# An encoder block on one core: a 320-byte tile ahead of the weights, and another order of the last sums and outputs

## The chip, the cores and the metric

The kernel runs on one core of a Trainium2 chip. The metric is the device time of one execution in microseconds (us); lower is better. The time before is 990.51 us, the median of three runs (989.64 to 991.15).

## The reference

One layer of an encoder over 256 tokens of width 2048, all in float32:

```python
h = rmsnorm(x, norm1_g)
proj = h @ w_in                               # q 1536 | k 512 | v 512 | u 512
a = rmsnorm(window_attention(q, k, v, sink), attn_out_g)   # 12 heads, 4 kv heads, |t-s| <= 128
f = rmsnorm(fourier_mix(u, w_fourier), fourier_out_g)
x = x + concatenate([a, f]) @ w_out
h = rmsnorm(x, norm2_g)
gate, val = split(h @ w_up)                   # 5504 columns each
gate = depthwise_conv3(gate, dw_w) + dw_b
x = x + (gelu(gate) * val) @ w_down
return rmsnorm(x, normf_g)
```

## The kernel before

**Products in two parts.** Every large product is made of float32 values split in two: `hi`, the value rounded to the type `float32r`, and `lo`, the rest. Three of the four partial products are summed: hi·hi, lo·hi and hi·lo. The tokens are kept turned and split, in four tiles `hT` of [128, 4, 512] (the tiles `hU` take their buffers after the first half of the layer): 256 columns hi and 256 columns lo side by side for each block of 128 features.

**Units.** The weights come in 24 units for `w_in` (4 for u, 4 for v, 16 for k and q), 16 for `w_out`, and for the feed-forward 86 for `w_up` (gate and value of 43 blocks of 128 columns) and 44 for `w_down` (11 groups of 4). A unit is 1 MB (768 KB in the last four), a tile of 128 partitions by 2048 float32. `load` issues its DMA from SyncE into one of three `raw` buffers; `split` makes `hi` on ScalarE (line 143) and `lo` on VectorE (line 144), two units ahead of TensorE.

**Two forms of matmul.** In `still_weights` (lines 293 and 294; k, q, gate, value) a unit's weights are the stationary operand. For each of 16 blocks there are two matmuls: `hi` against the 512 columns of a token tile, and `lo` against 256 columns of it. In `moving_weights` (lines 282 to 284; u, v, `w_out`, `w_down`) the weights stream, 512 columns at a time, and tokens, `cat` (the attention and Fourier outputs) or `act` (the activations) are stationary. A unit has 4 blocks, 2 token blocks and 3 partial products, so 24 matmuls. Each matmul instruction has its own weight load (PEld in the profile).

**Where tiles lie.** Pools are placed behind each other in the partitions of the on-chip memory, and tiles behind each other in their pool, with sizes rounded up to 32 bytes. `base` holds the residual `xs`, `hT` and small tiles; the weight pool `wp` (`raw`, `hi`, `lo`, `junk`) follows it, then `cat` and the attention's tiles, and in the feed-forward `fp` (with `act`) in their place. Each pair of one unit's operands is thus shifted against the other by the small tiles between them. Modulo 512 bytes, `hT` begins at 96 and `raw`, `hi`, `lo`, `cat` and `act` at 288.

**The end.** The order of instructions is written out by hand: each engine runs its own in the order of the code and waits for others through semaphores. The feed-forward alternates groups of 8 up units with 4 down units. The last down group has three blocks. Its eight products (column block c, token block b) come in the order (0,0), (0,1), (1,0), (1,1), (2,0), (3,0), (2,1), (3,1), the last in two halves of 256 columns (lines 941 to 943). `last_post` adds a product to the residual on VectorE (line 833), takes the sum of squares on ScalarE (`square_sum`, line 819) and, for c < 3, multiplies by the final gain on GpSimd (line 836). `most_of` adds the sums so far (`tot`, `part`), `last_scale` adds the last one (`var`) and takes the power -1/2 on GpSimd (`rstd`, line 854). `finish` scales the four column blocks of a token block, c = 0 and 1 on ScalarE (line 869), 2 and 3 on VectorE (lines 867 and 863), and issues their output DMAs from SyncE (line 870). `finish(0)` is recorded after product (2,1), ahead of the two halves of (3,1); `finish(1)` is last.

Of the kernel before, what the change touches and what calls it, by code (L numbers as in the profile page):

```python
# [8 lines left out]
F32 = mybir.dt.float32  # L9
F32R = mybir.dt.float32r  # L10
AF = mybir.ActivationFunctionType
ALU = mybir.AluOpType

P = 128
# [38 lines left out]
FF_GROUPS = [list(range(g * 4, min(g * 4 + 4, NF))) for g in range((NF + 3) // 4)]  # L53
# [3 lines left out]
def block_kernel(  # L57
# [17 lines left out]
    nc = tc.nc  # L75
    SL = slopes()
    ctx.enter_context(tc.manual_schedule())
    base = ctx.enter_context(tc.tile_pool(name="base", bufs=1))
# [7 lines left out]
    def bank(pool, name):  # L86
        return pool.tile([P, 512], F32, tag=pool.name, name=name)
# [24 lines left out]
    raws, halves = {}, {}  # L112
# [11 lines left out]
    def split(i, pieces=1):  # L124

        for _ in split_parts(i, pieces):
            pass
# [37 lines left out]
    xs = [base.tile([P, 2, 512], F32, tag=f"xs{c}", name=f"xs{c}") for c in range(4)]  # L165
# [60 lines left out]
    ps = bank(dn, "ps_warm")  # L226
# [49 lines left out]
    def moving_weights(hi, lo, n, kk, act, b, ps, first, last, q0=0):  # L276

        for q, k in enumerate(kk, q0):
            ah = act(k)[:, b * P : (b + 1) * P]
            al = act(k)[:, S + b * P : S + (b + 1) * P]  # L280
            wh, wl = hi[:, q * n : (q + 1) * n], lo[:, q * n : (q + 1) * n]
            nc.tensor.matmul(ps, ah, wh, start=first and q == q0, stop=False)  # L282
            nc.tensor.matmul(ps, al, wh, start=False, stop=False)  # L283
            nc.tensor.matmul(  # L284
                ps, ah, wl, start=False, stop=last and q == q0 + len(kk) - 1
            )
# [18 lines left out]
    def step(i, ahead=2):  # L305
        todo, later[:] = list(later), []
        for g in todo:
            next(g, None)
        split(i + ahead)
        for g in todo:  # L310
            for _ in g:
                pass
# [20 lines left out]
    for c in range(4):  # L333
        t = base.tile([P, 4, 512], F32R, tag=f"hT{c}", name=f"hT{c}")
        hT.append(t)
    ps_u = [bank(mm, f"ps_u{b}") for b in range(2)]
    for k in range(NK):
        c, q = k // 4, k % 4
# [4 lines left out]
        hi, lo = halves[c]  # L343
# [392 lines left out]
    for n, (c, kq) in enumerate(OUT_ORDER):  # L736
        i = N_OUT + n
# [14 lines left out]
        if kq >= 2:  # L752
            part = "a" if kq == 2 else "f"
            ps = ps_a[c] if kq < 3 else ps_a[c, "f"]
            last = c in added
# [15 lines left out]
    gfb = fp.tile([P, D], F32, tag="gfb", name="gfb", bufs=1)  # L771
    nc.gpsimd.dma_start(gfb, normf_g.partition_broadcast(P))
    hT[:] = hT2
    act = {}
# [42 lines left out]
    def square_sum(c, b, part, o, n):  # L817
        junk = wp.tile([P, 512], F32, tag="junk", name=f"junkc{c}{b}{part}")
        nc.scalar.activation(
            junk[:, 0:n], xs[c][:, b, o : o + n], AF.Square,  # L820
            accum_out=ssq3[:, b, part : part + 1],
        )

    def down_post(g, c, ps):
# [2 lines left out]
            nc.vector.tensor_tensor(xb, ps[b], xb, ALU.add)  # L827
        yield

    def last_post(c, b, ps, o=0, n=512, part=None):  # L830

        xb = xs[c][:, b, o : o + n]
        nc.vector.tensor_tensor(xb, ps, xb, ALU.add)
        square_sum(c, b, c if part is None else part, o, n)
        if c < 3:
            nc.gpsimd.tensor_tensor(
                xb, xb, gfb[:, c * 512 + o : c * 512 + o + n], ALU.mult
            )

    def most_of(b, n):  # L840

        tot = base.tile([P, 1], F32, tag=f"tot3{b}", name=f"tot3{b}")
        nc.vector.tensor_reduce(tot, ssq3[:, b, 0:n], mybir.AxisListType.X, ALU.add)
        var = base.tile([P, 1], F32, tag=f"part3{b}", name=f"part3{b}")
        nc.vector.tensor_scalar(var, tot, 1.0 / D, EPS, ALU.mult, ALU.add)
        return var

    def last_scale(b, n, var):
        v = base.tile([P, 1], F32, tag=f"var3{b}", name=f"var3{b}")
        nc.vector.scalar_tensor_tensor(  # L850
            v, ssq3[:, b, n : n + 1], 1.0 / D, var, ALU.mult, ALU.add
        )
        r = base.tile([P, 1], F32, tag=f"rstd3{b}", name=f"rstd3{b}")
        nc.gpsimd.tensor_tensor(r, v, half_pow[:, 0:1], ALU.pow)
        return r

    def finish(b, r):
        y = [
            fp.tile([P, 512], F32, tag="act", name=f"y{b}{c}", bufs=12) for c in range(4)
        ]  # L860
        for c in (0, 3, 1, 2):
            if c == 3:
                nc.vector.scalar_tensor_tensor(
                    y[c], xs[c][:, b, :], r, gfb[:, 1536:2048], ALU.mult, ALU.mult
                )
            elif c == 2:
                nc.vector.tensor_scalar(y[c], xs[c][:, b, :], r, None, ALU.mult)
            else:
                nc.scalar.activation(y[c], xs[c][:, b, :], AF.Copy, scale=r)
            nc.sync.dma_start(  # L870
                out[b * P : (b + 1) * P, c * 512 : (c + 1) * 512], y[c]
            )

    last = len(FF_GROUPS) - 1
    n = 0
    while n < len(ff_units):
        kind, g, j = ff_units[n]
        i = n_front + n
        if n == 0:
            pair = []  # L880
            for q in range(2):
                ps = bank(mm, f"ps_{ff_units[q][0]}{j}")
# [16 lines left out]
        hi, lo = halves.pop(i)  # L899
        if kind == "down" and g == last:  # L900
            break
        if kind == "down":
            ps = [bank(dn, f"ps_d{g}{j}{b}") for b in range(2)]
# [4 lines left out]
        else:  # L908
            ps = bank(mm, f"ps_{kind}{j}")
# [4 lines left out]


    halves[i] = (hi, lo)
    todo = []
    for c, b in [(0, 0), (0, 1), (1, 0), (1, 1), (2, 0), (3, 0), (2, 1), (3, 1)]:
        hi, lo = halves[i + c]
        ps = bank(dn, f"ps_e{c}{b}")  # L920
        if (c, b) != (3, 1):
            moving_weights(hi, lo, 512, FF_GROUPS[last], act.get, b, ps, True, True)
            todo.append((last_post, (c, b, ps)))
        if (c, b) in [(0, 1), (1, 0)]:
            step(i + c)
        if (c, b) != (0, 0):
            for f, a in todo:
                f(*a)
            todo = []
        if (c, b) == (3, 0):  # L930
            r3 = last_scale(0, 3, most_of(0, 3))
        if (c, b) == (2, 1):
            finish(0, r3)
    for p in range(2):
        ps = bank(dn, f"ps_e31{p}")
        for q, k in enumerate(FF_GROUPS[last]):
            o = q * 512 + p * 256
            ah, al = act[k][:, P:S], act[k][:, S + P : 2 * S]
            wh, wl = hi[:, o : o + 256], lo[:, o : o + 256]
            end = q == len(FF_GROUPS[last]) - 1  # L940
            nc.tensor.matmul(ps[:, 0:256], ah, wh, start=q == 0, stop=False)
            nc.tensor.matmul(ps[:, 0:256], al, wh, start=False, stop=False)
            nc.tensor.matmul(ps[:, 0:256], ah, wl, start=False, stop=end)
        last_post(3, 1, ps[:, 0:256], p * 256, 256, 3 + p)
        if p == 0:
            var = most_of(1, 4)
    finish(1, last_scale(1, 4, var))


def _layout(inp):  # L950
# [90 lines left out]
```

## Time and profile before

| | |
|---|---|
| median of three runs | 990.51 us (989.64 to 991.15) |
| the profiled execution's own time | 989.97 us |
| its span, first to last instruction | 988.2 us |
| granted TensorE clock, mean | 0.998 |
| TensorE busy | 977.0 us, 99% |
| weight loads busy | 838.2 us, 85% |
| VectorE, ScalarE, GpSimd busy | 696.1, 466.5, 23.6 us |
| DMA | 186.42 MB, mean 189 GB/s |

The profile names engines PE (TensorE), PEld (its weight loads), DVE (VectorE), ACT (ScalarE), POOL (GpSimd) and SP (SyncE). L12 is line 12 of the kernel. Tiles are given as out<-in. A row of the timeline has the start and the duration in us, the engine, the line, the operation, tiles, shapes and count, and in brackets the idle time before it and what ended it. A row of the view of stretches has the stretch, its length, and for each engine the busy time and in brackets the instructions.

### The profile page before, as it was taken

The page shows a single profiled execution, that of the slowest core. Times are in us where ns is not written, and L with a number is a line of the kernel's source. Part 1 is how long each engine was busy: PE and PEld are TensorE (multiplying, and loading weights), DVE is VectorE, ACT ScalarE, POOL GpSimd, SP SyncE. Part 2 cuts the span into 40 slices and gives each one's busy share as a digit, 9 for nine tenths or more (in the row PEclk, how much of TensorE's full clock was granted, in tenths as well). Part 3 has the DMA queues.
Part 4 walks back from the last instruction along what each step waited for, and adds up shares of the span by engine and source line. Part 5 has one row for each costly group of instructions (what it writes and reads, how often), then busy time and mean ns, then how long its engine had stood idle before and what let it go on. Part 6 is the DMA issues. An engine that isn't in the chain of part 4 may idle for free.

```text
span 988.2 us, 12858 instructions
## 1 busy us (share of the span) xinstructions
PE 977.0 (99%) x5185; PEld 838.2 (85%) x5185; DVE 696.1 (70%) x935; ACT 466.5 (47%) x587; POOL 23.6 (2%) x35
## 2 busy tenths in 40 slices
PE   9999999999999999999999999999999999999996
PEld 7788898888888888888888888888888888888885
DVE  6658877575687776767767767777677677676764
ACT  6756666544454434444434444344344343443434
POOL 0000000000000000000000000000000000000003
PEclk9999999999999999999999999999999999999999
DMA  9844443445545555464555555555545455555542
GB/s 330 341 178 153 148 165 134 171 170 205 221 170 178 204 178 206 172 213 171 191 192 180 204 182 201 184 196 177 210 170 208 175 192 192 178 206 190 193 128 86
DMA packets 30091, 186.42 MB, mean 189 GB/s; under 512 B 3408, under 2 KB 3920, under 8 KB 9040
## 3 DMA queue, kind: packets, MB, share of 16 engines
q1 hardware_dynamic: 29744, 184.54, 52.9%
q8 instruction: 41, 0.67, 0.3%
q0 software_dynamic: 144, 1.05, 0.3%
q14 instruction: 18, 0.15, 0.0%
q10 hardware_dynamic: 144, 0.01, 0.0%
HBM read 183.49 MB, written 2.10 MB: 188 GB/s over the span
## 4 chain that ended last, share of the span: by engine, by line
PE 98%; DMA 1%; issue 0%; SPq 0%; ACT 0%; POOL 0%; DVE 0%; ACTq 0%; POOLq 0%
PE ps_gate L293 16%; PE ps_val L293 16%; PE ps_val L294 8%; PE ps_gate L294 8%; PE ps_d L284 7%; PE ps_d L283 7%; PE ps_d L282 7%; PE ps_q L293 5%; PE ps_q L294 2%; PE ps_a L284 2%; PE ps_a L282 2%; PE ps_a L283 2%; PE ps_k L293 2%; PE ps_o L642 1%; PE ps_s L570 1%; PE ps_k L294 1%
## 5 line engine op out<-in xcount | busy, mean ns | idle before, releaser
L144 DVE TENSOR_TENSOR lo<-raw,hi 128x2048 fp32r<-128x2048 f32 (+3 forms) x178 | 388.4, 2182 | 97.7 <-ACT hi L143 97.7
L143 ACT ACTIVATE hi<-raw 128x2048 fp32r<-128x2048 f32 (+3 forms) x177 | 324.3, 1832 | 166.6 <-PE ps_d L283 106.0
L293 PE MATMUL ps_gate<-hU,hi 128*128 128x512 f32 x688 | 242.6, 394 | 0.0
L293 PE MATMUL ps_val<-hU,hi 128*128 128x512 f32 x688 | 242.6, 394 | 0.0
L294 PE MATMUL ps_val<-hU,lo 128*128 128x256 f32 x688 | 193.0, 281 | 0.0
L294 PE MATMUL ps_gate<-hU,lo 128*128 128x256 f32 x688 | 193.0, 280 | 0.0
L293 PEld LDWEIGHTS ps_val<-hU,hi 128*128 128x128 f32 x688 | 129.4, 188 | 30.1
L293 PEld LDWEIGHTS ps_gate<-hU,hi 128*128 128x128 f32 x688 | 129.4, 188 | 30.0
L294 PEld LDWEIGHTS ps_gate<-hU,lo 128*128 128x128 f32 x688 | 128.9, 187 | 0.4
L294 PEld LDWEIGHTS ps_val<-hU,lo 128*128 128x128 f32 x688 | 128.9, 187 | 0.0
L284 PE MATMUL ps_d<-lo,act 128*128 128x512 f32 x320 | 124.6, 389 | 0.0
L283 PE MATMUL ps_d<-hi,act 128*128 128x512 f32 x320 | 124.6, 389 | 0.0
L282 PE MATMUL ps_d<-hi,act 128*128 128x512 f32 x320 | 124.5, 389 | 0.0
L780 ACT ACTIVATE ft_g<-ps_gate 128x256 f32<-128x256 f32 x43 | 16.5, 384 | 134.2 <-PE ps_gate L294 134.2
L827 DVE TENSOR_TENSOR xs<-ps_d,xs 128x512 f32<-128x512 f32 x80 | 54.5, 687 | 25.7 <-PE ps_d L284 25.7
L282 PEld LDWEIGHTS ps_d<-hi,act 128*128 128x128 f32 x320 | 60.1, 188 | 12.6
L284 PEld LDWEIGHTS ps_d<-lo,act 128*128 128x128 f32 x320 | 60.1, 188 | 12.5
L283 PEld LDWEIGHTS ps_d<-hi,act 128*128 128x128 f32 x320 | 60.1, 188 | 12.2
L293 PE MATMUL ps_q<-hT,hi 128*128 128x512 f32 x192 | 68.5, 397 | 0.0
L780 ACT ACTIVATE ft_v<-ps_val 128x256 f32<-128x256 f32 x43 | 16.5, 384 | 95.5 <-PE ps_val L294 95.5
L782 DVE TENSOR_TENSOR fa_g<-ps_gate,ft_g 128x256 f32<-128x256 f32 x43 | 18.2, 424 | 55.3 <-ACT ft_g L780 55.3
L294 PE MATMUL ps_q<-hT,lo 128*128 128x256 f32 x192 | 54.0, 281 | 0.0
(175 smaller groups left out, 1036.1 us busy)
## 6 DMA issues: line engine op xcount, KB each, us to landing
raw<-in_w_up SPq DMA_DIRECT2D x86, 1024.0 KB, 4.8
raw<-in_w_down SPq DMA_DIRECT2D x40, 1024.0 KB, 4.7
raw<-in_w_in SPq DMA_DIRECT2D x21, 1024.0 KB, 4.9
raw<-in_w_out SPq DMA_DIRECT2D x16, 1024.0 KB, 4.8
raw<-in_w_down_last SPq DMA_DIRECT2D x4, 768.0 KB, 4.2
raw<-in_w_in SPq DMA_DIRECT2D x8, 256.0 KB, 5.7
xs<-in_x SPq DMA_DIRECT2D x4, 512.0 KB, 10.8
out_y<-y SPq DMA_DIRECT2D x8, 256.0 KB, 2.5
```

The source lines that it names most:

```text
L143: nc.scalar.activation(hi[:, s], raw[:, s], AF.Copy)
L144: nc.vector.tensor_tensor(lo[:, s], raw[:, s], f32(hi[:, s]), ALU.subtract)
L282: nc.tensor.matmul(ps, ah, wh, start=first and q == q0, stop=False)
L283: nc.tensor.matmul(ps, al, wh, start=False, stop=False)
L284: nc.tensor.matmul(ps, ah, wl, start=False, stop=last and q == q0 + len(kk) - 1)
L293: nc.tensor.matmul(ps, hi[:, s], h, start=k == 0, stop=False)
L294: nc.tensor.matmul(ps[:, 0:S], lo[:, s], h[:, 0:S], start=False, stop=k == NK - 1)
L570: nc.tensor.matmul(ps[:, b * S : (b + 1) * S], qT[:, qo + b * P : qo + (b + 1) * P], kT[:, ko : ko + S], start=n == 0, stop=n == 2,)
L642: nc.tensor.matmul(ps[:, 0:S], v[:, sb, g * HD : (g + 1) * HD], pt[q][:, sb * S : (sb + 1) * S], start=sb == 0 and n == 0, stop=sb == 1 an ...
L780: nc.scalar.activation(tmp, ps[:, S : 2 * S], AF.Copy)
L782: nc.vector.tensor_tensor(add, ps[:, 0:S], tmp, ALU.add)
L827: nc.vector.tensor_tensor(xb, ps[b], xb, ALU.add)
```

## The change

1. A tile of 320 bytes a partition, `room`, is allocated in `base` behind the four token tiles. No instruction uses it. All tiles behind it move by 320 bytes, so the tokens stay at 96 modulo 512, and `raw`, `hi`, `lo`, `cat` and `act` begin at 96 as well.
2. The multiplication by the final gain becomes a function of its own, `gain`. `finish` becomes a generator that records one output at a time, in the order c = 0, 3, 2, 1. For token block 0, outputs 0 and 3 are recorded after product (2,1), output 2 after the first half of (3,1), and output 1 after the second half and after `most_of`. `most_of(1)` is recorded after the second half's addition and square instead of between the halves.

The order of TensorE's and GpSimd's instructions stays. The loop over the last products is written out.

```diff
+    base.tile([P, 80], F32, tag="room", name="room")
...
+    def gain(c, b):
+        xb = xs[c][:, b, :]
+        nc.gpsimd.tensor_tensor(xb, xb, gfb[:, c * 512 : (c + 1) * 512], ALU.mult)
...
         square_sum(c, b, c if part is None else part, o, n)
-        if c < 3:
-            nc.gpsimd.tensor_tensor(
-                xb, xb, gfb[:, c * 512 + o : c * 512 + o + n], ALU.mult
-            )
...
-        for c in (0, 3, 1, 2):
+        for c in (0, 3, 2, 1):
...
             nc.sync.dma_start(
                 out[b * P : (b + 1) * P, c * 512 : (c + 1) * 512], y[c]
             )
+            yield
...
+    r3 = last_scale(0, 3, most_of(0, 3))
+    last_post(2, 1, last_product(2, 1))
+    outs = finish(0, r3)
+    next(outs)
+    next(outs)
+    gain(2, 1)
+    hi, lo = halves[i + 3]
     for p in range(2):
...
         last_post(3, 1, ps[:, 0:256], p * 256, 256, 3 + p)
         if p == 0:
-            var = most_of(1, 4)
-    finish(1, last_scale(1, 4, var))
+            next(outs)
+    most = most_of(1, 4)
+    for _ in outs:
+        pass
+    for _ in finish(1, last_scale(1, 4, most)):
+        pass
```

More of the change, by code (lines that the diff above doesn't have):

```diff
@@ L916, in block_kernel, with last_product @@
     halves[i] = (hi, lo)
-    todo = []
-    for c, b in [(0, 0), (0, 1), (1, 0), (1, 1), (2, 0), (3, 0), (2, 1), (3, 1)]:
+    def last_product(c, b):
         hi, lo = halves[i + c]
         ps = bank(dn, f"ps_e{c}{b}")
[L921 to L933, printed above, removed]
+        moving_weights(hi, lo, 512, FF_GROUPS[last], act.get, b, ps, True, True)
+        return ps
+    held_ps = last_product(0, 0)
+    ps = last_product(0, 1)
+    step(i)
+    last_post(0, 0, held_ps)
+    last_post(0, 1, ps)
+    gain(0, 0)
+    gain(0, 1)
+    ps = last_product(1, 0)
+    step(i + 1)
+    last_post(1, 0, ps)
+    gain(1, 0)
+    for c, b in [(1, 1), (2, 0), (3, 0)]:
+        last_post(c, b, last_product(c, b))
+        if c < 3:
+            gain(c, b)
+    r3 = last_scale(0, 3, most_of(0, 3))
[5 more added lines that the diff above has]
+    hi, lo = halves[i + 3]
     for p in range(2):
```

## The prediction

> **What bounds the kernel now.** I read the page first (busy shares, slices, chain), then the busy time of each engine in chosen stretches, then the timeline of the last microseconds.
>
> ```profile
> PE 977.0 (99%) x5185; PEld 838.2 (85%) x5185; DVE 696.1 (70%) x935; ACT 466.5 (47%) x587; POOL 23.6 (2%) x35
> ...
> PEclk9999999999999999999999999999999999999999
> ...
> PE 98%; DMA 1%; issue 0%; SPq 0%; ACT 0%; POOL 0%; DVE 0%; ACTq 0%; POOLq 0%
> ```
>
> TensorE is busy 977.0 of the 988.2 us, at full clock in every slice, and is 98% of the chain that ended last. There is hardly a wait to remove. The time can only fall if matmuls follow each other at a shorter spacing, or if the part after the last matmul gets shorter. The change tries both: a 320-byte tile that moves operands in memory, and a new order of the last vector and scalar steps.
>
> For the first part I need the true spacing from one matmul's start to the next; the mean durations don't give it, since matmuls are pipelined and overlap in the trace. So I chose stretches that begin with the first matmul of a stage and end with the first of the next, and divide their length by the matmuls that the code issues in them.
>
> ```profile
> core 0: us, PE busy (x) PEld busy (x) DVE busy (x) ACT busy (x) POOL busy (x), PEclk, DMA share, GB/s
> 29.41:40.61 11.20, 11.20 (x50) 8.97 (x48) 3.71 (x4) 10.51 (x21) 0.71 (x1) 1.00 1.03 403
> 50.78:56.37 5.59, 5.59 (x27) 4.51 (x25) 2.95 (x2) 2.88 (x3) 0.00 (x0) 1.00 0.34 139
> 486.50:508.29 21.79, 21.79 (x99) 18.02 (x98) 15.21 (x15) 8.28 (x7) 0.00 (x0) 1.00 0.57 196
> 508.29:552.95 44.66, 44.66 (x258) 39.11 (x256) 32.42 (x41) 19.79 (x22) 0.00 (x0) 1.00 0.53 188
> 274.38:353.61 79.23, 79.23 (x452) 68.96 (x451) 62.66 (x84) 37.78 (x46) 0.00 (x0) 1.00 0.53 186
> 89.21:94.85 5.64, 5.64 (x35) 4.92 (x33) 5.25 (x16) 3.67 (x8) 0.00 (x0) 1.00 0.55 189
> ```
>
> Rows one and two are v units, row three four down units, rows four and five up units, row six one q unit. Put beside them where the operands lie. The allocator gives each tile a place in its partition; modulo 512 bytes, before the change, tokens (hT, hU) are at 96, and weights (hi, lo), the attention outputs (cat) and the activations (act) at 288. Each slice a matmul reads starts a multiple of 512 bytes further, so it has the same place.
>
> - Down (row three): 512 columns, both operands at 288. 21.79 us for 4 units of 24 matmuls: **227.0 ns** each.
> - v (rows one and two): the same instruction form, 512 columns, but tokens at 96 against weights at 288. 11.20 us / 48 = **233.3 ns** and 5.59 / 24 = **232.9 ns**. The two rows differ threefold in DMA (403 and 139 GB/s) and much in ScalarE (94% and 52% busy), and the spacing is the same. So it isn't traffic of others; what differs from down is which tiles are read, and where they lie.
> - Up and q: a 512-column matmul (tokens times hi) and a 256-column one (times lo), tokens at 96, weights at 288. 44.66 / 128 pairs = **348.9 ns**; in the first groups 79.23 / 224 = **353.7 ns**; in q 5.64 / 16 = **352.5 ns**.
>
> **Part 1, the 320 bytes.** `room` lies in the pool behind the tokens and ahead of the weights. Tokens stay at 96; weights, cat and act go from 288 to 96 (288 + 320 = 608). So after it the operands of u, v, q, k and up have one place, as those of down and of the output projection have now, and those of down and projection still have one place. Nothing is added to any engine. In the Fourier and attention parts nearly all pairs of tiles move together. What the landing places of the loads cost DMA is covered: its share is 0.53 to 0.57 in the feed-forward.
>
> The cost of a pair with one place isn't in the trace, since no stage mixes 512 and 256 columns at one place. I build it from its halves. The 512-column half is down's, 227.0 ns. For 256 columns at one place there are the last 18 matmuls (act and hi, both at 288):
>
> ```profile
> 976.55 0.28 PE L941 MATMUL ps_e<-hi,act 128*128 128x256 f32 x1
> 976.66 0.28 PE L942 MATMUL ps_e<-hi,act 128*128 128x256 f32 x1
> ...
> 978.58 0.28 PE L943 MATMUL ps_e<-lo,act 128*128 128x256 f32 x1
> ```
>
> From the second to the eighteenth 1.92 us for 16: 120.0 ns. The first follows a 512-column matmul and takes 0.11 us only. I take 120.0, from sixteen, and keep 0.113 for the range. Pair: 227.0 + 120.0 = **347.0 ns**.
>
> - 16 up units in the slow rhythm: 256 pairs x (353.7 - 347.0) = 1.7 us.
> - The other 70: 1120 x (348.9 - 347.0) = 2.1 us.
> - 16 q and k units: 256 x (352.5 - 347.0) = 1.4 us.
> - 8 u and v units: 192 matmuls x (232.9 - 227.0) = 1.1 us. I count half, 0.6: in the first v stretch ScalarE is 10.51 of 11.20 us busy and DMA at share 1.03, so they end next there.
>
> Sum **5.8 us**. In up nothing is late next: VectorE, the next busiest, works 32.42 of 44.66 us.
>
> The Trainium skill speaks against all of this: "TensorE: Matmul & The Clock Gate", Step-by-step, says that TensorE has two independent read ports, and that loading the next weights takes no read bandwidth from the running matmul. By it the relative place of the two operands would cost nothing, and this part would bring 0 instead of 5.8 us. The rows disagree so far: 232.9 and 233.3 ns against 227.0 with only tiles and places different.
>
> **Part 2, the end.** These rows carry it (the last matmul starts at 978.58, above):
>
> ```profile
> 977.36 0.74 DVE L863 SCALAR_TENSOR_TENSOR y<-xs,rstd,gfb 128x512 f32<-128x512 f32 x1
> 978.02 0.48 DVE L867 TENSOR_SCALAR y<-xs,rstd 128x512 f32<-128x512 f32 x1
> 978.17 1.32 ACT L869 ACTIVATE y<-xs,rstd 128x512 f32<-128x512 f32 x2
> 978.34 1.29 POOL L836 TENSOR_TENSOR xs<-xs,gfb 128x512 f32<-128x512 f32 x1 [1.17 <-ACT junkc L819]
> 978.41 0.42 DVE L833 TENSOR_TENSOR xs<-ps_e,xs 128x256 f32<-128x256 f32 x1
> 978.90 4.23 SPq L870 DMA_DIRECT2D out_y<-y  x5
> 979.39 0.40 ACT L819 ACTIVATE junkc<-xs 128x256 f32<-128x256 f32 x1
> 979.70 0.18 ACT L819 ACTIVATION_READ_ACCUMULATOR junkc<-xs 128x1 f32 x1
> 979.92 0.16 DVE L843 TENSOR_REDUCE tot<-ssq 128x1 f32<-128x4 f32 x1 [1.09 <-ACT junkc L819]
> 980.11 0.15 DVE L845 TENSOR_SCALAR part<-tot 128x1 f32<-128x1 f32 x1
> 980.18 0.41 DVE L833 TENSOR_TENSOR xs<-ps_e,xs 128x256 f32<-128x256 f32 x1
> 980.69 0.42 ACT L819 ACTIVATE junkc<-xs 128x256 f32<-128x256 f32 x1 [0.80 <-DVE xs L833]
> 981.23 0.16 DVE L850 SCALAR_TENSOR_TENSOR var<-ssq,part 128x1 f32<-128x1 f32 x1 [0.64 <-ACT junkc L819]
> 981.47 0.56 POOL L854 TENSOR_TENSOR rstd<-var,half_pow 128x1 f32<-128x1 f32 x1 [1.84 <-DVE var L850]
> 982.06 1.34 ACT L869 ACTIVATE y<-xs,rstd 128x512 f32<-128x512 f32 x2 [0.86 <-POOL rstd L854]
> ...
> L870 SPq DMA_DIRECT2D out_y<-y x8: 332/399/451, 978.9 to 984.2; - x8
> ```
>
> The last product is over by 978.86, but its addition (second L833) starts at 980.18. It stands behind the sum of squares (tot, part), which waits for ScalarE's square at 979.39, which stands behind two outputs of the first block (978.17, 1.32). The change takes one of these two outputs (c = 1) out of ScalarE's way and puts it behind both squares; on VectorE it orders: first addition, output c = 2, last addition, then tot and part. Replayed with the same durations:
>
> - VectorE: output c = 3 as now; first addition at 978.02; output c = 2 at 978.41; last addition at about 978.95, over at 979.36.
> - ScalarE: output c = 0 from 978.17 to 978.83; square of the first half to about 979.4; square of the second 0.1 us behind its addition (as 980.59 to 980.69 now), at 979.46; its sum reaches VectorE 0.54 us later (as 980.69 to 981.23): var at 980.00.
> - tot and part fit in from 979.43 to 979.75, ahead of that.
>
> var comes at 980.0 instead of 981.23: **1.2 us**. The moved output is then on ScalarE from 979.98 to 980.64; the scale of the second block (0.83 us behind var's start, 981.23 to 982.06) comes at 980.83. It hides by 0.2 us; without that cover the end slips by at most 0.66. Its DMA leaves SP's queue at 980.7 for some 0.4 us, ahead of the second block's first issue near 981.6. The multiplication by the gain on GpSimd (978.34, 1.29) keeps its place in its queue and is over at 979.63, before the power. The exchange of c = 1 and c = 2 in the second block changes nothing: four issues in a row set the end there, the last at 984.2, whichever tile comes third.
>
> **Sum.** 5.8 + 1.2 = 7.0 us. Against the profiled execution, 989.97 us: 983.0. That run lies 0.5 us under the median of 990.51, so the forecast is **983.5 us**.
>
> **The rivals.**
>
> 1. *The short matmuls gain too.* If the pair keeps the 113 ns that the first short matmul behind a long one shows, it is 340 ns: 7.0 x 1632 pairs = 11.4 us more, 972.1. For: that one spacing is just the change of length that up makes in each pair. Against: it is one of seventeen, and may be what is left of the run before. Chance 0.12.
> 2. *One rhythm alone.* The places only bring the slow rhythm (353.7, 352.5) to the fast one (348.9): 512 pairs x about 4.2 = 2.1, with 0.6 and 1.2: 3.9 us, 986.6. For: both occur at the same places now, so what a stretch starts with counts as well. Chance 0.08.
> 3. *The places cost nothing*; v is slower than down for another reason, and the end alone gains: 989.3, no difference that can be measured. Against: two v stretches with unlike neighbours agree within 0.4 ns. Chance 0.11. The rule of the Trainium skill cited in part 1 comes to the same.
> 4. *Slower: each place counts by itself.* If weights loaded from 96 cost 6 ns a matmul wherever the streamed operand lies (in v the loaded tile is the tokens at 96, in down it is act at 288), the change brings that to all: 960 down, 384 projection and 63 last matmuls, 1407 x 6 = 8.4 us, and the 1632 long matmuls of up, q and k, whose loaded tile goes from 288 to 96 too, up to 9.8 us. Less the 1.2 of the end: 997.7 with down's alone, 1007.5 with both. It decides as soon as the difference to down comes from the loaded side alone. Against: up loads from 288 already, and a pair there still costs 348.9 to 353.7, over 227.0 + 120.0. Chance 0.07.
>
> That the operands don't move as said is no rival: the places follow from the order and sizes of the allocations.
>
> **How the numbers follow.** The forecast has 0.62; its own range is 981 to 986 (the pair from 346 to 348.5, u and v at nothing or in full, the end at 0.5 to 1.2 us). About 0.2% (2.0 us) is what a measurement here can tell from no change. Faster: forecast, rivals 1 and 2, 0.82; within 0.2%: rival 3, 0.11; slower: rival 4, 0.07. A range of 974.0 to 989.5 holds the forecast, rivals 2 and 3, and rival 1 with up to 9.5 of its 11.4 us, but not rival 1 in full, nor rival 4.
>
> **What would show it.** In the trace of after: v at 227 ns; eight up units in 44.4 us instead of 44.66, and the first fourteen in 77.7 instead of 79.23; four down units still 21.79. The last var 1.4 us behind the last matmul's start instead of 2.65. Wrong if up keeps 348.9 or v 233 (rival 3), wrong in sign if down's stretch grows towards 22.4.

## The result

The changed kernel takes **995.12 us** (median of five, 994.50 to 996.17) against 990.51 (989.64 to 991.66): ratio **1.0047, 95% interval 1.0032 to 1.0061**. It is slower by 4.6 us; the forecast was 983.5, in a range of 974.0 to 989.5.

The page of the changed kernel shows as full a TensorE as before, for longer:

```profile
span 994.4 us, 12859 instructions
...
PE 982.9 (99%) x5185; PEld 838.0 (84%) x5185; DVE 697.8 (70%) x935; ACT 466.5 (47%) x587; POOL 23.5 (2%) x35
```

These are the stretches of before at their new places: u, v, v, four down units, eight up units, the first fourteen, a q unit.

```profile
4.88:31.45 26.57, 25.04 (x98) 17.17 (x97) 18.42 (x28) 16.29 (x27) 0.00 (x0) 1.00 0.99 359
31.45:42.33 10.88, 10.88 (x50) 9.01 (x48) 3.66 (x4) 10.47 (x21) 0.71 (x1) 1.00 0.98 388
52.41:57.88 5.47, 5.47 (x26) 4.52 (x25) 2.96 (x2) 2.88 (x3) 0.00 (x0) 1.00 0.38 156
489.18:511.00 21.82, 21.82 (x98) 18.02 (x97) 15.25 (x15) 8.27 (x7) 0.00 (x0) 1.00 0.57 195
511.00:556.21 45.21, 45.21 (x257) 39.19 (x256) 32.42 (x41) 19.79 (x22) 0.00 (x0) 1.00 0.53 186
275.89:355.11 79.22, 79.22 (x451) 68.71 (x450) 62.66 (x84) 37.80 (x46) 0.00 (x0) 1.00 0.53 186
90.75:96.39 5.64, 5.64 (x34) 4.90 (x33) 5.26 (x16) 3.67 (x8) 0.00 (x0) 1.00 0.56 189
```

- v gains as forecast: 10.88 / 48 = 226.7 ns (233.3 before) and 5.47 / 24 = 227.9 (232.9).
- Up loses: 45.21 / 128 = **353.2 ns** a pair where it was 348.9, and 347.0 was forecast. The first fourteen units (79.22, 79.23 before) and q (5.64 both) stay. Nearly all pairs of up now take about the slow rhythm that those had already.
- Down is nearly still: 21.82 against 21.79.

So 1120 pairs x 4.3 ns = 4.8 us come from up, the whole result and a little more. The profiled execution (996.17 us, the longest of the five) has 2 us more in the u units at the start, where DMA is the limit (share 0.99). That isn't the places: the same stretch took

```profile
4.80:29.41 24.61, 23.72 (x99) 17.71 (x99) 18.16 (x28) 16.35 (x27) 0.00 (x0) 1.00 1.00 378
```

before, and in the first experiment, with the places of the changed kernel,

```profile
5.29:30.16 24.87, 24.23 (x98) 18.19 (x98) 17.95 (x28) 16.08 (x27) 0.00 (x0) 1.00 0.99 368
```

The end of the changed kernel, in its timeline:

```profile
984.63 0.42 DVE L839 TENSOR_TENSOR xs<-ps_e,xs 128x256 f32<-128x256 f32 x1
984.95 1.27 POOL L834 TENSOR_TENSOR xs<-xs,gfb 128x512 f32<-128x512 f32 x1 [1.15 <-ACT junkc L821]
984.96 1.54 DVE L869 TENSOR_SCALAR y<-xs,rstd 128x512 f32<-128x512 f32 x1
985.19 0.28 PE L958 MATMUL ps_e<-lo,act 128*128 128x256 f32 x1
985.39 0.40 ACT L821 ACTIVATE junkc<-xs 128x256 f32<-128x256 f32 x1
986.42 0.41 DVE L839 TENSOR_TENSOR xs<-ps_e,xs 128x256 f32<-128x256 f32 x1
986.93 0.42 ACT L821 ACTIVATE junkc<-xs 128x256 f32<-128x256 f32 x1 [1.05 <-DVE tot L845]
987.47 0.16 DVE L852 SCALAR_TENSOR_TENSOR var<-ssq,part 128x1 f32<-128x1 f32 x1 [0.38 <-ACT junkc L821]
```

The order is the forecast one, and ScalarE takes both squares ahead of the moved output. But VectorE's output c = 2 takes 1.54 us, where it took 0.48; it began with GpSimd's multiplication and ended just behind it. The last addition waits for it until 986.42, and var starts 2.28 us behind the last matmul's start (2.65 before, 1.4 forecast): a gain of 0.4 us.

### The profile page after: what moved, and what is told of

Its sections match the earlier page's. It is cut to its first block, busy times and chain, and to the rows that moved or that the text cites. A ratio compares the mean times of both kernels' runs of the same rounds, so it can differ in the third digit from the quotient of the medians.

```text
span 994.4 us, 12859 instructions
## 1 busy us (share of the span) xinstructions
PE 982.9 (99%) x5185; PEld 838.0 (84%) x5185; DVE 697.8 (70%) x935; ACT 466.5 (47%) x587; POOL 23.5 (2%) x35
## 4 chain that ended last, share of the span: by engine, by line
PE 96%; DMA 2%; SPq 0%; ACT 0%; DVE 0%; issue 0%; POOL 0%; ACTq 0%; POOLq 0%
PE ps_gate L293 16%; PE ps_val L293 16%; PE ps_val L294 8%; PE ps_gate L294 8%; PE ps_d L282 7%; PE ps_d L284 7%; PE ps_d L283 7%; PE ps_q L293 5%; PE ps_q L294 2%; PE ps_a L284 2%; PE ps_a L282 2%; PE ps_a L283 2%; DMA raw<-in_w_in 2%; PE ps_k L293 2%; PE ps_s L572 1%; PE ps_o L644 1%
```

## The experiments

**e1 and e2: each half alone.** e1 is the kernel before with `room`, e2 the kernel before with the new end.

> The kernel before with the 320-byte tile alone. Theory A (the places set the pace of up): with everything at one place a pair of up takes 353 ns instead of 348.9, u and v gain about 1 us: 994 to 997 us. Theory B (the new order of the end costs the time): no more than 1 us from 990.5. If the u units were slow by chance in the changed kernel's profile, they take about 24.6 us here, not 26.6.

> The kernel before with the new order of the end alone. Theory A: about 0.4 us faster than before, 990.1, since GpSimd's multiplication and VectorE's output c = 2 still meet (that output takes 1.5 us instead of 0.5). Theory B: 4 to 5 us slower. If the end gains the 1.2 us forecast where nothing else moved: 989.3.

e1: 995.29 us, 1.0043 (1.0029 to 1.0057). e2: 990.19 us, 0.9994 (0.9986 to 1.0003), the slow output again 1.54 us. The tile alone makes the loss; the end alone can't be told from no change. Theory A holds on both, and the u units of e1 are at 24.87 us.

**e3 and e4: long and short matmuls in runs.** In each up, q and k unit the sixteen 512-column matmuls come first, then the sixteen of 256; e3 with the change, e4 without.

```diff
         for k in kk:
             ...
             nc.tensor.matmul(ps, hi[:, s], h, start=k == 0, stop=False)
+        for k in kk:
+            ...
             nc.tensor.matmul(
                 ps[:, 0:S], lo[:, s], h[:, 0:S], start=False, stop=k == NK - 1
             )
```

> The changed kernel with the matmuls of up, q and k sorted in each unit: the 16 long ones (512 columns), then the 16 short ones (256 columns). Theory A1 (it is the alternation of long and short at one place that costs): a pair falls to 227.0 + 120.0 = 347 ns, 1632 pairs x 6.2 = 10 us less than the changed kernel, 985 us. Theory A2 (up pays for its operands at one place in any order): 995 us as the changed kernel.

> The kernel before, tokens at 96 and weights at 288, with the same sorting. If long runs at unlike places cost 233 ns a long matmul, as u and v did, a pair takes 233 + 120 = 353 ns: 995 us. If sorting alone is what helps, whatever the places: 985 us.

e3: **986.19 us**, 0.9951 (0.9938 to 0.9963). e4: **982.50 us**, 0.9913 (0.9899 to 0.9926). Timeline of a gate unit of e3, merged by line, up to the next unit's first row:

```profile
505.90 3.79 PE L293 MATMUL ps_gate<-hU,hi 128*128 128x512 f32 x16
509.52 2.08 PE L297 MATMUL ps_gate<-hU,lo 128*128 128x256 f32 x16
511.44 0.40 PE L293 MATMUL ps_val<-hU,hi 128*128 128x512 f32 x1
```

3.62 / 16 = 226 ns long, 1.92 / 16 = 120 short: the halves that the prediction used, within a nanosecond. This unit is the first behind a down group; in later ones the long matmuls take 228 ns (3.65 / 16, from 865.17), the short ones 120. So the halves hold in runs, while the groups behind down of the changed kernel, which alternate, take 353.2 a pair. But the halves can add up in alternation too. In the changed kernel's first value and gate units, behind eight small matmuls (`ps_x`), there are 17 alternating pairs between these two rows:

```profile
269.29 0.39 PE L293 MATMUL ps_val<-hU,hi 128*128 128x512 f32 x1
...
275.18 0.39 PE L293 MATMUL ps_val<-hU,hi 128*128 128x512 f32 x1
```

5.89 / 17 = **346.5 ns**, at the same places as the 353.2. Matmuls of other kinds cut up, q and k into 28 alternating stretches of 12 to 224 pairs, and in each trace a stretch keeps one rhythm from its first few pairs to its end. With one place, 5 of the 28 run at about 347 ns (the same 5 in e1) and 23 at 353, among these all 9 behind a down group. In the kernel before, 14 run at 349, among these the same 9, and 14 at 353. So at one place alternation isn't dearer in itself: the tile moved the stretches behind down from the faster rhythm at one distance to the slower one at another.

In e4:

```profile
503.67 3.84 PE L293 MATMUL ps_gate<-hU,hi 128*128 128x512 f32 x16
507.35 1.98 PE L297 MATMUL ps_gate<-hU,lo 128*128 128x256 f32 x16
509.16 0.39 PE L293 MATMUL ps_val<-hU,hi 128*128 128x512 f32 x1
```

230 ns long, but 113 short; in the value units 229 (3.66 / 16, from 860.86) and 118 (1.89 / 16). So A1 gives the time of e3, and for e4 both expectations missed: the long runs in up don't cost the 233 ns of v, although tokens and weights lie as far apart in both, and the short runs are cheaper than at one place. The roles differ: in v the tokens are loaded and the weights stream, in up it is the reverse. That suggested a distance with a sign.

**The places.** Six kernels with other sizes of `room`, or with it ahead of the tokens. Up groups with j below 24 alternate, the later ones are in runs, so one trace shows both. The cuts are against the kernel before. Each kernel ran once; what is compared are stretches of the traces, not the times (987.54 to 993.38 us).

```diff
-    def still_weights(hi, lo, ps, kk):
+    def still_weights(hi, lo, ps, kk, sort=False):
...
+    base.tile([P, 16], F32, tag="room", name="room")     # 16, 32, 48, 64 or 112
...
-            still_weights(hi, lo, ps, range(NK))
+            still_weights(hi, lo, ps, range(NK), j >= 24)
```

> From here on the kernels have the old end, up groups 1 to 6 (j below 24) alternating as before and the later ones sorted, so that one profile shows both forms. Here the 320-byte tile lies ahead of the tokens: everything from the tokens on moves by 320 bytes, and weights stay 192 bytes past the tokens modulo 512. Theory R (only the distance counts): all as in the kernel before, v 233 ns, alternating pairs 348.9 in the steady groups, sorted as in e4 (long about 229, short 113 to 118 ns). Theory P (each place counts by itself): v or up change by 4 ns or more.

> The tile behind the tokens has 448 bytes: weights 128 past the tokens modulo 512. If only an equal place modulo 512 is special, v takes 233 ns, alternating pairs 349, sorted long 229. If the distance counts modulo 128, all is as at distance 0: v 227, alternating 353, sorted long 227 and short 120.

> 192 bytes: weights 384 past the tokens. Modulo 512: v 233, alternating 349, sorted long 229. Modulo 128: as at distance 0, v 227, alternating 353, sorted 227 and 120. If this differs from distance 128, the sign counts too, and v, where tokens are loaded and weights stream, shows the other sign.

> 256 bytes: weights 448 past the tokens, 64 modulo 128 as in the kernel before (192). Both rules expect the numbers of before: v 233, alternating 349 in the steady groups, sorted long 229, short 113 to 118.

> 64 bytes behind the tokens: weights 256 past them modulo 512, alternating groups first, sorted ones later. If the distance counts modulo 256, this is distance 0 although no two tiles begin at one place modulo 512: v 227 ns, alternating pairs 353, sorted long 227 and short 120. If it counts modulo 512, anything else.

> 128 bytes: weights 320 past the tokens, 64 modulo 256. If what counts is the loaded operand's place minus the streamed one's modulo 256, long matmuls in a row take 229.3 ns at 192 and 233 at 64, in whichever stage: here v (tokens loaded, weights streamed, so 192) falls to 229.3 and up's sorted long ones (64) rise to 233, the reverse of the kernel before. If the stage counts and not the sign, v stays at 233 and up at 229.

In the view of stretches, each time one v unit, eight alternating up units and eight in runs. All moved, distance still 192:

```profile
50.76:56.35 5.59, 5.59 (x27) 4.51 (x25) 2.96 (x2) 2.88 (x3) 0.00 (x0) 1.00 0.41 167
442.11:486.77 44.66, 44.66 (x257) 39.11 (x256) 32.43 (x41) 19.80 (x22) 0.00 (x0) 1.00 0.53 187
839.25:883.39 44.14, 44.14 (x257) 38.82 (x256) 32.42 (x41) 19.79 (x22) 0.00 (x0) 1.00 0.55 190
```

Distance 448:

```profile
50.80:56.42 5.62, 5.62 (x26) 4.50 (x25) 2.95 (x2) 2.88 (x3) 0.00 (x0) 1.00 0.46 179
441.88:486.54 44.66, 44.66 (x257) 39.11 (x256) 32.43 (x41) 19.81 (x22) 0.00 (x0) 1.00 0.53 187
839.02:883.16 44.14, 44.14 (x257) 38.82 (x256) 32.42 (x41) 19.80 (x22) 0.00 (x0) 1.00 0.54 190
```

Distance 128:

```profile
52.43:58.01 5.58, 5.58 (x26) 4.53 (x25) 2.95 (x2) 2.88 (x3) 0.00 (x0) 1.00 0.28 113
442.99:487.92 44.93, 44.93 (x258) 39.37 (x257) 32.42 (x41) 19.79 (x22) 0.00 (x0) 1.00 0.54 186
843.41:888.39 44.98, 44.98 (x258) 39.27 (x256) 32.42 (x41) 19.78 (x22) 0.00 (x0) 1.00 0.53 186
```

Distance 384:

```profile
50.77:56.35 5.58, 5.58 (x26) 4.53 (x25) 2.95 (x2) 2.88 (x3) 0.00 (x0) 1.00 0.48 192
441.33:486.26 44.93, 44.93 (x258) 39.38 (x257) 32.43 (x41) 19.79 (x22) 0.00 (x0) 1.00 0.53 186
841.75:886.73 44.98, 44.98 (x258) 39.27 (x256) 32.41 (x41) 19.78 (x22) 0.00 (x0) 1.00 0.52 186
```

Distance 256:

```profile
51.07:56.54 5.47, 5.47 (x26) 4.51 (x25) 2.95 (x2) 2.88 (x3) 0.00 (x0) 1.00 0.42 172
442.62:487.83 45.21, 45.21 (x257) 39.24 (x256) 32.41 (x41) 19.79 (x22) 0.00 (x0) 1.00 0.53 185
842.60:887.11 44.51, 44.51 (x258) 39.37 (x257) 32.41 (x41) 19.80 (x22) 0.00 (x0) 1.00 0.53 188
```

Distance 320, and one of its gate units in the timeline up to the next unit's first row:

```profile
51.81:57.32 5.51, 5.51 (x26) 4.52 (x25) 2.96 (x2) 2.88 (x3) 0.00 (x0) 1.00 0.34 141
443.78:489.00 45.22, 45.22 (x257) 39.26 (x256) 32.43 (x41) 19.80 (x22) 0.00 (x0) 1.00 0.53 185
843.30:887.68 44.38, 44.38 (x257) 38.60 (x256) 32.40 (x41) 19.79 (x22) 0.00 (x0) 1.00 0.52 189
```

```profile
865.50 3.89 PE L293 MATMUL ps_gate<-hU,hi 128*128 128x512 f32 x16
869.22 1.98 PE L298 MATMUL ps_gate<-hU,lo 128*128 128x256 f32 x16
871.04 3.89 PE L293 MATMUL ps_val<-hU,hi 128*128 128x512 f32 x16
```

Divided by 24 matmuls of v and 128 pairs of up, always in groups behind a down group (distance 0 with the rows of the changed kernel too):

| weights past tokens, modulo 256 bytes | kernels | v, ns each | up alternating, ns a pair | up in runs, ns a pair |
|---|---|---|---|---|
| 0 | changed; 256 | 227.9; 227.9 | 353.2; 353.2 | 347.7 |
| 64 | 320 | 229.6 | 353.3 | 346.7 |
| 128 | 128; 384 | 232.5; 232.5 | 351.0; 351.0 | 351.4; 351.4 |
| 192 | before; all moved; 448 | 232.9; 232.9; 234.2 | 348.9; 348.9; 348.9 | 344.8; 344.8 (the latter two) |

Only the distance counts: with all tiles moved by 320 bytes, v and the groups of up stay (theory R). The four q and k units that ran at 349 ns in the kernel before run at 353 here, so the rhythm of a stretch doesn't hang on the distance alone. Among these distances, all multiples of 64, it counts modulo 256 bytes: 128 and 384, 192 and 448 give the same up to a hundredth of a microsecond in eight up units, and 256 gives what one place gives. The expectations of both "modulo 512 alone" and "modulo 128" fell. And the sign counts: at 320 v falls to 229.6 and up's long run rises to 3.72 / 16 = 232.5 ns, as expected of 64 and 192 with their roles exchanged.

**k1 and k2: the end on top of e4.** k1 is e4 with the new end. k2 takes GpSimd out of the second block's column block 2:

```diff
-            if c == 3:
+            if c == 3 or (c, b) == (2, 1):
                 nc.vector.scalar_tensor_tensor(
-                    y[c], xs[c][:, b, :], r, gfb[:, 1536:2048], ALU.mult, ALU.mult
+                    y[c], xs[c][:, b, :], r, gfb[:, c * 512 : (c + 1) * 512],
+                    ALU.mult, ALU.mult,
                 )
...
-    gain(2, 1)
```

> Sorted units at the places of before, with the new order of the end. The end as it came gains 0.4 us: 982.1 us, and the last var starts about 2.3 us behind the last matmul's start. If the 1.2 us forecast come where the rest is unmoved: 981.3 and 1.4 us.

> As k1, but column block 2 of the second token block is multiplied by the final gain in its output on VectorE (one scalar_tensor_tensor, as column block 3 is) instead of ahead of it on GpSimd. Theory C (GpSimd's multiplication holds up VectorE's output c = 2): that output takes 0.5 us instead of 1.5, the last var starts about 1.4 us behind the last matmul's start, 981.2 us. Rival (that output is slow because of ScalarE or DMA beside it): 1.5 us stays, and the time is that of k1.

k1: 981.91 us, 0.9913 (0.9900 to 0.9927). k2: **981.48 us**, 0.9912 (0.9898 to 0.9925). The two medians are too close to call, the traces aren't: in k1 var starts 2.27 us behind the last matmul's start. k2:

```profile
970.81 0.48 DVE L871 TENSOR_SCALAR y<-xs,rstd 128x512 f32<-128x512 f32 x1
971.05 0.28 PE L959 MATMUL ps_e<-lo,act 128*128 128x256 f32 x1
971.36 0.42 DVE L840 TENSOR_TENSOR xs<-ps_e,xs 128x256 f32<-128x256 f32 x1
972.42 0.16 DVE L853 SCALAR_TENSOR_TENSOR var<-ssq,part 128x1 f32<-128x1 f32 x1 [0.31 <-ACT junkc L822]
```

Without GpSimd beside it the output takes 0.48 us, and var starts 1.37 us behind, the forecast replay to 0.05. Theory C is shown. k2 has the lowest median of all kernels here, 8.8 us under its runs of before.

## Why the prediction was wrong, step by step

- **"Pair: 227.0 + 120.0 = 347.0 ns"** is the step that failed, and it alone turns the sign. The prediction took the sum of the halves for the price of a pair at one place. The changed kernel does have that pair, at 346.5 ns, but only in 5 of its 28 alternating stretches; the 9 stretches behind down groups run in the slower rhythm, at 353.2, where they ran at 348.9 before. The trace of before held a warning: the same code at the same places ran at 348.9 and at 353.7, so the place alone doesn't set the price. The prediction named what a stretch starts with in rival 2 alone, and compared stretches of both lengths at unlike places with stretches of one length at one place. Two of its counts were rough as well: 12 of the 256 pairs counted as slow, and most pairs of four of the 16 q and k units, ran at 349 already, which is worth about 0.3 of the 5.8 us.
- **The relative place counts** held: v fell from 232.9 to 227.9, and with all moved it stayed at 232.9. The Trainium skill's rule of independent read ports for streamed operand and weights ("TensorE: Matmul & The Clock Gate", Step-by-step) isn't borne out as a rule on time: moving the weights against the tokens changes the spacing of v by 5 to 7 ns in 233. But that an equal place is the cheapest held only for long matmuls in a row. Short ones in a row are cheaper at 192 (113 and 118 ns) or 64 (114) than at 0 (120), and alternation behind a down group is cheapest at 192, where the kernel stood.
- **u and v, 0.6 us**: the two v stretches gained 0.32 and 0.12 us, the first although ScalarE and DMA were full beside it. For u no gain can be told: its stretch took 24.27 (e3) to 26.57 us (changed kernel) at one place, and 24.61 in the kernel before.
- **Rival 4** (slower, each place by itself) got the sign and not the mechanism: down stayed at 21.82. **Rival 2** expected the places to bring the slow rhythm to the fast one; in the groups behind down they did the reverse. Its remark that what a stretch starts with counts as well is borne out.
- **The end, 1.2 us,** gave 0.4 in the trace. The terms of the replay were right save one: "output c = 2 at 978.41", taken at 0.48 us. The replay moved it by 0.4 us and so into GpSimd's multiplication. In before its row started at 978.02, ahead of GpSimd's at 978.34. The prediction looked only at whether GpSimd's step is over before the power. In the changed kernel GpSimd's starts 0.01 us ahead, and the output takes 1.54 us; without GpSimd beside it, in k2, it takes 0.48. The Trainium skill has a rule for this: "SBUF — State Buffer", SBUF: two separate sides, has VectorE, in some of its operations, and GpSimd share a port pair that one of them holds for a whole instruction while the other is blocked. The traces agree in that the output waits; it ends 0.28 us behind GpSimd's multiplication (986.50 against 986.22), which is sooner than a full 0.48 after it.

Open: why two of the four distances, 0 and 192, have two rhythms, while every stretch at 64 (about 353 ns) and at 128 (about 351) runs in one, what in the start of a stretch chooses between them (behind `ps_y` alone, both occur at one place), why a pair in the slower one costs more than its halves, and what repeats every 256 bytes. The runs give the sizes, not the mechanism.

## What to carry to other kernels

Where matmuls with their own weight loads bound a kernel, the order of long and short ones and the distance of the two operands in a partition, modulo 256 bytes, are worth some tenths of a per cent to a per cent; measure the pattern as it runs and behind the work that it follows, not its parts in other patterns. Here sorting alone, one loop made two, brought 8 us, while none of the places tried made alternating groups behind down faster than before. When a step on VectorE is moved, look at what GpSimd does at the new time, and not only at who waits for whom.

## What the runs showed of the hardware that was not expected

- The spacing of matmuls repeats with the operands' distance modulo 256 bytes, with a sign (loaded against streamed operand): long matmuls in v take 228 ns with the weights 0 past the tokens, 229.6 at 64, 232.5 at 128 and 232.9 at 192 (234.2 at distance 448).
- Alternating lengths run in one of two rhythms at the same places, and a stretch keeps the one it starts with, for up to 224 pairs: 346.5 or 353.2 ns a pair at one place, 348.9 or 353.7 at 192.
- Behind a down group, alternation at one place costs 353.2 ns a pair against 347.7 in runs; at 128 it is no dearer (351.0 and 351.4).
- A VectorE output of 128x512 takes 0.48 us alone and 1.54 us beside a GpSimd multiplication of 1.27 us that starts 0.01 us ahead of it. Started 0.32 us ahead of GpSimd's, in the kernel before, it takes 0.48 as well.
